# One ScalarE copy for all readers of a product bank in the block inverse of a gated DeltaNet layer

## The chip, the core and the metric

The kernel runs on one core of a Trainium2 chip. The metric is device time in microseconds (us), the median of several executions; lower is better. The core has five engines that run side by side, each through its own queue in order: TensorE (PE; its weight loads are shown as PEld), VectorE (DVE), ScalarE (ACT), GpSimd (POOL) and SyncE (SP), which issues the DMAs. They meet at semaphores.

## The reference

One decoder layer on 2048 tokens of width 1024: a gated DeltaNet mixer with 8 heads in chunks of 64 tokens and a memory attention with 4 heads, one output projection, a layer norm, a squared-ReLU MLP of width 4096, a second layer norm. What matters here is the triangular solve of each chunk:

```python
decay = jnp.exp(jnp.where(causal, gc[..., :, None] - gc[..., None, :], -jnp.inf))
lower = jnp.where(strict, jnp.einsum('bnhcd,bnhsd->bnhcs', k_beta, kc) * decay, 0.0)
a_mat = jnp.eye(CHUNK, dtype=f32) + lower
u = lax.linalg.triangular_solve(a_mat, v_beta, left_side=True, lower=True, unit_diagonal=True)
w = lax.linalg.triangular_solve(a_mat, k_beta * jnp.exp(gc)[..., None], left_side=True,
                                lower=True, unit_diagonal=True)
...
def step(state, inp):
    qd, kd, u_c, w_c, a_c, dc = inp
    v_new = u_c - jnp.einsum('bhcd,bhde->bhce', w_c, state)
    o = jnp.einsum('bhcd,bhde->bhce', qd, state) + jnp.einsum('bhcs,bhse->bhce', a_c, v_new)
    state = state * dc[..., None, None] + jnp.einsum('bhcd,bhce->bhde', kd, v_new)
    return state, o
```

The kernel inverts the unit lower triangular matrix itself, in chunks of 128 tokens, instead of solving twice.

## The kernel before

The tokens are cut into four blocks of 512 (`TB`), each of which holds four chunks (`NC`) of 128 rows. For two blocks at a time the program runs the mixer of each block, the output projection (`out_seven`), and the MLP (`ff1`, `ff2`) with one level of Strassen's scheme. A mixer goes over the 8 heads: `dense` projects q, k and v, `gdn_a` builds the chunks' matrices and calls `invert`, `gdn_b` runs the recurrence over the state. So there are 4 x 8 = 32 calls of `invert`. Head t's projections, head t-1's inverse and head t-2's recurrence are recorded in one turn of the loop, together with the gates, the memory heads and sums of weights for the MLP.

Nothing is issued where it is written. Every call goes into a `Recorder` (L190), which notes for each operation the earlier operations that it depends on: a write against earlier readers and writers of the same tile, a read against earlier writers, told apart by `part` keys and, in SBUF, by partitions and columns (`Ref.mask`). Two reads of one tile make no edge there. `Recorder.cost` (L250) gives each operation a time, `LAT`, `LAT_FROM` and `MARGIN` (L33 to L35) the hand-over between engines, and `Recorder.issue` (L291) plays the engines' queues as a list scheduler: of the operations that are ready on an engine it takes the one recorded first. The order that comes out is the order in which the engines get their instructions; the semaphores are placed afterwards by the framework from what the tiles share. A tile's name in the profile is the name given to it in the code; most lines are that of the one call in `issue` (L402), so groups are told apart by tiles.

`invert` (L851) takes L, four chunks of 128 x 128 whose strictly lower triangle counts, and returns the inverse in Y. It builds up from blocks of 16 to 32 to 64 to 128 rows:

- `Lq` holds the four 32 x 32 diagonal blocks of each chunk, copied by ScalarE from L with the chunk index innermost; two VectorE operations make `Lc` of it, and 15 steps of three VectorE operations each (`B`, `Xc`) eliminate within the blocks of 16. `ZT` and `Z` are the result and its transpose.
- First product pair, blocks of 16: `pq` = LB x ZT, copied to `Q`; `pp` = XB x Q, subtracted from `ZT`.
- `ZP`, the first 64 columns of the same tile `Lq`, receives packed blocks of ZT. `X32` and `X64` (in the `inv` tiles, which are zero outside their blocks) receive the diagonal blocks of Z: of four copies for each, GpSimd makes two and VectorE two. ScalarE copies ZT's diagonal blocks into Y.
- Second pair, blocks of 32: `pq` = L32 x ZP, copied to Q; `pb` (the bank `pp`) = X32 x Q. This bank has five readers: a VectorE transpose of its upper half into the second half of `Lq`, two VectorE multiplications by -1 and two ScalarE activations with scale -1, each of a 32 x 64 block into Y. Two VectorE multiplications by -1 carry the transposed blocks into X64.
- Third pair, blocks of 64: `YP` is packed from Y by one VectorE and one ScalarE copy; `pq` = LP x YP, copied to Q; `pp` = X64 x Q, whose two halves VectorE and ScalarE write, negated, into Y.

`gdn_a` goes on with the transposes of v, and `gdn_b` multiplies by Y.

The bank of each product is one tile of a PSUM pool (`ga0` or `ga1` by the head's parity, one buffer each).

Of the kernel before, what the change touches and what calls it, by code (L numbers as in the profile page):

```python
# [10 lines left out]
AF = mybir.ActivationFunctionType  # L11
# [3 lines left out]
P = 128  # L15
TB = 512
NC = TB // P
# [14 lines left out]

LAT = {("PE", "PE"): 0, ("DVE", "POOL"): 190, ("ACT", "POOL"): 215, ("PE", "POOL"): 350, ("DVE", "DVE"): 130, ("ACT", "ACT"): 155, ("POOL", "POOL"): 100}  # L33
LAT_FROM = {"PE": 200, "DVE": 130, "ACT": 135, "POOL": 75, "SP": 60}
MARGIN = 100  # L35
DRAIN, SWITCH = {"DVE": 90, "ACT": 100, "POOL": 98}, 0


# [145 lines left out]

class Op:
    __slots__ = ("i", "eng", "fn", "args", "kw", "dur", "extra", "succ", "npred", "ready", "start", "end", "load", "last",
                 "bufs", "prio", "quads", "cols", "late", "lhs")


class Recorder:  # L190
# [15 lines left out]
    def add(self, eng, fn, name, args, kw):  # L206
        o = Op()
        o.i, o.eng, o.fn, o.args, o.kw = len(self.ops), eng, fn, args, kw
        o.succ, o.npred, o.ready, o.extra = [], 0, 0, 0
        o.prio = o.i + self.shift  # L210
        wr = [v for k, v in kw.items() if k in ("out", "accum_out")]
        rd = [v for k, v in kw.items() if k not in ("out", "accum_out")]
        rest = list(args)
        if "out" not in kw and rest:
            wr.append(rest.pop(0))
        rd += rest
        wr = [v for v in wr if isinstance(v, Ref)]
        rd = [v for v in rd if isinstance(v, Ref)]
        o.dur = self.cost(o, name, wr, rd, args, kw)

        o.quads = {("r" if v in rd else "w", v.buf.psum): v.p0 // 32 for v in wr + rd[::-1]}
        preds = {}
        for refs, is_w in ((rd, False), (wr, True)):
            for r in refs:
                parts, free = r.mask()
                for q, qw, qk, qp, qf in r.buf.log:
                    if (is_w or qw) and (qk is None or r.keys is None or qk & r.keys) and qp & parts and qf & free:
                        preds[q.i] = q
        for refs, is_w in ((rd, False), (wr, True)):
            for r in refs:  # L230
                log = r.buf.log
                parts, free = r.mask()
                if is_w:
                    log[:] = [e for e in log if not ((e[2] == r.keys or r.keys is None) and e[3] & ~parts == 0
                                                     and e[4] & ~free == 0)]
                log.append((o, is_w, r.keys, parts, free))
        if eng == "SP" and self.gate is not None:
            preds[self.gate.i] = self.gate
        for q in preds.values():
            q.succ.append(o)  # L240
        o.npred = len(preds)
        o.bufs = list({id(r.buf): r.buf for r in rd + wr}.values())
        for b in o.bufs:
            if b.first is None:
                b.first = o.i
            b.users += 1
        self.ops.append(o)
# [43 lines left out]
    def issue(self):  # L291
# [7 lines left out]
        quads, cols = {e: {} for e in DRAIN}, P  # L299
# [40 lines left out]
        out = []  # L340
        fed = 0.0
        while True:
# [3 lines left out]
            for e in engs:  # L346
                if avail[e]:
                    t = free[e]
                elif soon[e]:
                    t = max(free[e], soon[e][0][0])  # L350
# [6 lines left out]
            t, e = best  # L357
            while soon[e] and soon[e][0][0] <= t:
                r, i, o = heapq.heappop(soon[e])
                heapq.heappush(avail[e], (o.prio, i, o))  # L360
            o = heapq.heappop(avail[e])[2]
            if e == "PE":
                if o.cols != cols:
                    t += SWITCH
                    cols = o.cols
                t = max(t, fed + o.load)
                fed = t + o.dur - o.last
            if e in DRAIN:
                at = quads[e]
                if any(at.get(k, q) != q for k, q in o.quads.items()):  # L370
                    t = max(t, free[e] + DRAIN[e])
# [7 lines left out]
            for s in o.succ:  # L379
                lat = LAT.get((e, s.eng), LAT_FROM[e])  # L380
                if e == "PE" and lat and o.last < 60:
                    lat += 65 if o.last > 30 else 130
                if lat:
                    lat += MARGIN + (s.load if s.eng == "PE" and s.lhs in o.bufs else 0)
                s.ready = max(s.ready, o.end + lat)
                s.npred -= 1
                if s.npred == 0:
                    pending.append(s)
# [30 lines left out]
def hybrid_layer(  # L419
# [24 lines left out]
    nc = tc.nc  # L444
# [21 lines left out]
    def small(name, shape, bufs=3, dt=F32):  # L466
        return rec.buf(sm, shape, dt, name, bufs, name)
# [15 lines left out]
    half = cst.tile([P, 2], F32, name="half")  # L483
# [21 lines left out]
    nc = rec  # L505
# [344 lines left out]

    def invert(L, par):  # L851

        Lq = small("Lq", [P, 32, NC], 2)
        for q in range(4):
            r = slice(32 * q, 32 * q + 32)
            nc.scalar.copy(out=Lq[r].rearrange("p f c -> p c f"), in_=L[r, :, 32 * q:32 * q + 32])
            nc.gpsimd.tensor_copy(inv["LB"][r, :, r].rearrange("p u (k f) -> p u k f", k=2),
                                  L[r, :, 32 * q:32 * q + 16].rearrange("p (k u) f -> p u k f", k=2))
        L32, LP = inv["L32"], inv["LP"]
        for p in range(2):  # L860
# [4 lines left out]
        nc.gpsimd.tensor_copy(LP[64:, :, :64].part(0), L[64:, 0:2, :64])  # L865
        nc.vector.tensor_copy(LP[:64, :, 64:].part(1), L[64:, 2:4, :64])
        Lc = small("Lc", [P, 16, NC], 2)
        nc.vector.tensor_scalar_mul(Lc, Lq[:, 0:16], half[:, 0:1])
        nc.vector.scalar_tensor_tensor(out=Lc, in0=Lq[:, 16:32], scalar=half[:, 1:2], in1=Lc,
                                       op0=ALU.mult, op1=ALU.add)  # L870
        Xc = small("Xc", [P, 16, NC], 2)
        nc.vector.tensor_copy(Xc, i16.unsqueeze(2).to_broadcast([P, 16, NC]))
# [1 line left out]
        for j in range(15):  # L874
# [3 lines left out]
                                    in1=Lc[:, j:j + 1].to_broadcast([P, w, NC]), op=ALU.mult)  # L878
            nc.vector.tensor_tensor(out=Xc[:, :w], in0=Xc[:, :w], in1=B[:, :w], op=ALU.subtract)
        Z = small("Z32", [P, NC, 32], 2)  # L880
        for hf in range(2):
# [6 lines left out]
                                       in1=Z[:, 0:2, 0:16], op0=ALU.mult, op1=ALU.add)  # L888
# [25 lines left out]
        nc.vector.tensor_tensor(out=zt, in0=zt, in1=pp.rearrange("p (u k f) -> p u k f", u=2, k=2), op=ALU.subtract)  # L914


        ZP = Lq.rearrange("p f c -> p (f c)")[:, :64].rearrange("p (c f) -> p c f", c=2)
        Z = small("Z32", [P, NC, 32], 2)
        for p in range(2):
            odd = slice(64 * p + 32, 64 * p + 64)  # L920
# [1 line left out]
            nc.scalar.copy(out=ZP[odd].part(2 * p), in_=ZT[odd, 0:2])  # L922
        nc.vector.transpose(Z.rearrange("p c f -> p (c f)"), ZT.rearrange("p c f -> p (c f)"))
        for p in range(2):
            for u, eng in ((0, nc.gpsimd), (1, nc.vector)):
                q = quads[2 * p + u]
                eng.tensor_copy(X32[q, :, q].part((u, p)), Z[64 * p:64 * p + 32, 2 * u:2 * u + 2])
        for p in range(2):
            for u, eng in ((0, nc.gpsimd), (1, nc.vector)):
                q = quads[2 * u + p]  # L930
                eng.tensor_copy(X64[q, :, q].part((u, p)), Z[quads[p], 2 * u:2 * u + 2])
        for r in quads:
            nc.scalar.copy(out=Y3[r, :, r], in_=ZT[r])

# [5 lines left out]
        pp = pb.rearrange("p (c f) -> p c f", c=2)  # L940
        for c in range(2):
            nc.tensor.matmul(pp[:, c], X32[:, c], Q[:, 64 + c * 32:64 + (c + 1) * 32].part(1), start=True, stop=True)
        tr = Lq.rearrange("p f c -> p (f c)")[:64, 64:].part("t")
        nc.vector.transpose(tr, pb[:64])
        for p in (1, 0):
            o = Y3[64 * p:64 * p + 32, :, 64 * p + 32:64 * p + 64]
            nc.vector.tensor_scalar_mul(o[:, 2:4], pp[quads[2 * p + 1]], -1.0)
            nc.scalar.activation(o[:, 0:2], pp[quads[2 * p]], AF.Copy, scale=-1.0)
        tr = tr.rearrange("p (c f) -> p c f", c=2)
        for u in range(2):  # L950
            nc.vector.tensor_scalar_mul(X64[quads[2 * u + 1], :, quads[2 * u]].part((u, 2)), tr[quads[u]].part("t"), -1.0)

        YP = small("YP", [P, 2, 64], 1)
        nc.vector.tensor_copy(YP[:64].part(1), Y3[64:, 2:4, 64:])
# [874 lines left out]
```

## Time and profile before

| what | before |
|---|---|
| median of the runs | 2762.95 us (2762.62 to 2763.29, 3 runs) |
| the profiled execution | 2760.71 us |
| its span, first to last instruction | 2759.0 us |
| mean granted TensorE clock | 0.997 |
| HBM read / written | 436.54 / 174.65 MB |

The span is what the profile shows; the time of an execution has a little around it. In the profile, busy times are those in which an engine worked on an instruction of the program, and "idle before" is the time an engine stood still just before an instruction, with the instruction that released it behind the arrow. A group's row gives out <- in by the names of the tiles, the shape, the count, the busy time and the mean of one in ns. In a timeline, the first column is the start, the second the duration of that instruction or run of instructions. A busy TensorE is not one at its peak, since its matmuls are pipelined and their ends are modelled.

### The profile page before, as it was taken

The page shows a single profiled execution, that of the slowest core. Times are in us where ns is not written, and L with a number is a line of the kernel's source. Part 1 is how long each engine was busy: PE and PEld are TensorE (multiplying, and loading weights), DVE is VectorE, ACT ScalarE, POOL GpSimd, SP SyncE. Part 2 cuts the span into 40 slices and gives each one's busy share as a digit, 9 for nine tenths or more (in the row PEclk, how much of TensorE's full clock was granted, in tenths as well). Part 3 has the DMA queues.
Part 4 walks back from the last instruction along what each step waited for, and adds up shares of the span by engine and source line. Part 5 has one row for each costly group of instructions (what it writes and reads, how often), then busy time and mean ns, then how long its engine had stood idle before and what let it go on. Part 6 is the DMA issues. An engine that isn't in the chain of part 4 may idle for free.

```text
span 2759.0 us, 42405 instructions
## 1 busy us (share of the span) xinstructions
PE 2719.8 (99%) x13589; PEld 2267.0 (82%) x13589; DVE 2112.2 (77%) x5652; ACT 1642.3 (60%) x4082; POOL 403.7 (15%) x1030
## 2 busy tenths in 40 slices
PE   9999999999999999999999999999999999999998
PEld 7888888887788888888888888888887788888887
DVE  7889889998777777665778887888978665657575
ACT  7678767676485556334446676677855655544342
POOL 3233223321000000000023321223201000000000
PEclk9999999999999999999999999999999999999999
DMA  8565558876788888766754344444578744477673
GB/s 327 207 234 205 215 182 288 290 258 228 269 284 302 280 285 297 268 211 205 265 209 149 138 155 174 169 147 159 206 251 280 249 145 152 163 252 243 205 239 116
DMA packets 208543, 613.99 MB, mean 223 GB/s; under 512 B 23072, under 2 KB 32192, under 8 KB 188352
## 3 DMA queue, kind: packets, MB, share of 16 engines
q1 hardware_dynamic: 207888, 611.23, 63.5%
q8 instruction: 107, 1.75, 0.2%
q14 instruction: 116, 0.95, 0.1%
q10 hardware_dynamic: 432, 0.05, 0.0%
HBM read 436.54 MB, written 174.65 MB: 222 GB/s over the span
## 4 chain that ended last, share of the span: by engine, by line
PE 88%; ACT 7%; DVE 4%; issue 1%; POOL 1%; DMA 0%; DVEq 0%; SPq 0%; POOLq 0%; ACTq 0%
PE f2A L402 13%; PE fA L402 12%; PE ao L402 8%; PE f2C L402 6%; PE fC L402 6%; PE az L402 5%; PE aq L402 5%; PE av L402 5%; PE ak L402 5%; PE f2B L402 3%; PE fB L402 3%; PE amq L402 3%; PE pc L402 3%; PE po L402 2%; PE pkq L402 1%
## 5 line engine op out<-in xcount | busy, mean ns | idle before, releaser
L402 DVE TENSOR_TENSOR whl<-wraw,whl 128x512 fp32r<-128x512 f32 (+2 forms) x294 | 257.2, 884 | 109.4 <-ACT whl L402 107.0
L402 ACT CAST whl<-wraw 128x512 fp32r<-128x512 f32 (+2 forms) x294 | 226.5, 780 | 158.0 <-PE fC L402 52.0
L402 PE MATMUL fA<-B,whl 128*128 128x512 f32 x1152 | 277.2, 389 | 1.8 <-ACT B L402 1.5
L402 ACT CAST X<-X 128x1024 fp32r<-128x1024 f32 x118 | 123.9, 1052 | 236.2 <-DMA X<-xsc 196.2
L402 PE MATMUL f2A<-whl,X 128*128 128x512 f32 x1152 | 262.1, 389 | 0.0
L402 PEld LDWEIGHTS fA<-B,whl 128*128 128x128 f32 x1152 | 216.1, 188 | 47.5 <-ACT B L402 1.9
L402 PEld LDWEIGHTS f2A<-whl,X 128*128 128x128 f32 x1152 | 216.2, 188 | 44.9
L402 DVE TENSOR_TENSOR X<-X,X 128x1024 fp32r<-128x1024 f32 x118 | 144.2, 1223 | 129.0 <-ACT X L402 128.8
L402 PE MATMUL aq<-T,whl 128*128 128x512 f32 x768 | 214.3, 408 | 10.0 <-ACT T L402 5.5
L402 PE MATMUL az<-T,whl 128*128 128x512 f32 x768 | 213.0, 406 | 0.0
L402 PE MATMUL ak<-T,whl 128*128 128x512 f32 x768 | 211.4, 406 | 0.0
L402 PE MATMUL av<-T,whl 128*128 128x512 f32 x768 | 210.4, 404 | 0.0
L402 PE MATMUL fC<-B,whl 128*128 128x512 f32 x768 | 185.4, 389 | 0.3 <-DVE B L402 0.3
L402 PE MATMUL f2C<-whl,X 128*128 128x512 f32 x768 | 174.7, 389 | 0.0
L402 PEld LDWEIGHTS fC<-B,whl 128*128 128x128 f32 x768 | 144.1, 188 | 30.7 <-DVE B L402 0.8
L402 PEld LDWEIGHTS f2C<-whl,X 128*128 128x128 f32 x768 | 144.1, 188 | 29.9
L402 PEld LDWEIGHTS aq<-T,whl 128*128 128x128 f32 x768 | 136.5, 191 | 32.7 <-ACT T L402 5.5
L402 POOL TENSOR_SCALAR ve<-mv 128x1 f32<-128x1 f32 x34 | 16.4, 483 | 962.0 <-DVE mv L402 961.5
L402 PEld LDWEIGHTS av<-T,whl 128*128 128x128 f32 x768 | 137.3, 189 | 22.7
L402 PEld LDWEIGHTS ak<-T,whl 128*128 128x128 f32 x768 | 136.4, 189 | 23.5
L402 PEld LDWEIGHTS az<-T,whl 128*128 128x128 f32 x768 | 135.9, 189 | 21.6
L402 PE MATMUL ao<-whl,X 128*128 128x512 f32 x528 | 140.1, 404 | 3.5 <-DVE whl L402 1.3
(287 smaller groups left out, 6300.8 us busy)
## 6 DMA issues: line engine op xcount, KB each, us to landing
whl<-wsc SPq DMA_DIRECT2D x108, 1024.0 KB, 4.8
wraw<-in_w_ff_dram SPq DMA_DIRECT2D x106, 512.0 KB, 4.5
X<-xsc SPq DMA_DIRECT2D x96, 512.0 KB, 3.9
wsc<-whl SPq DMA_DIRECT2D x36, 1024.0 KB, 5.2
whl<-tsc SPq DMA_DIRECT2D x64, 512.0 KB, 4.7
xsc<-hB SPq DMA_DIRECT2D x96, 256.0 KB, 3.4
xo<-cat SPq DMA_DIRECT2D x80, 256.0 KB, 3.9
wraw<-in_w_in_dram SPq DMA_DIRECT2D x35, 512.0 KB, 5.9
```

Source lines behind the costliest of these rows:

```text
L402: o.fn(*[res(a) for a in o.args], **{k: res(v) for k, v in o.kw.items()})
```

## The change

Five things are changed.

1. `Lq` gets the chunk index outermost, so that ScalarE's copies into it are contiguous; `Lc` is made from a permuted view `Lf` of it.
2. The four copies of Z's diagonal blocks into `X32` are all VectorE's, the four into `X64` all GpSimd's.
3. The bank `pb` has one reader, a ScalarE activation with scale -1 that writes all of it into the second half of `Lq` (`Nf`). The transpose (now into the first half, where ZP was), the two VectorE and the two ScalarE copies into Y read that; they and the two copies into X64 are plain copies without a factor.
4. In the recorder, a read of a PSUM tile gets an edge from each earlier read of it by another engine, if there is none yet (`turns`).
5. In the scheduler such an edge counts 40 ns (`TURN`) after the earlier reader's end.

```diff
--- before.py
+++ after.py
@@ -32,7 +32,7 @@
 
 LAT = {("PE", "PE"): 0, ("DVE", "POOL"): 190, ("ACT", "POOL"): 215, ("PE", "POOL"): 350, ("DVE", "DVE"): 130, ("ACT", "ACT"): 155, ("POOL", "POOL"): 100}
 LAT_FROM = {"PE": 200, "DVE": 130, "ACT": 135, "POOL": 75, "SP": 60}
-MARGIN = 100
+MARGIN, TURN = 100, 40
 DRAIN, SWITCH = {"DVE": 90, "ACT": 100, "POOL": 98}, 0
 
 
@@ -184,7 +184,7 @@
 
 class Op:
     __slots__ = ("i", "eng", "fn", "args", "kw", "dur", "extra", "succ", "npred", "ready", "start", "end", "load", "last",
-                 "bufs", "prio", "quads", "cols", "late", "lhs")
+                 "bufs", "turns", "prio", "quads", "cols", "late", "lhs")
 
 
 class Recorder:
@@ -206,7 +206,7 @@
     def add(self, eng, fn, name, args, kw):
         o = Op()
         o.i, o.eng, o.fn, o.args, o.kw = len(self.ops), eng, fn, args, kw
-        o.succ, o.npred, o.ready, o.extra = [], 0, 0, 0
+        o.succ, o.npred, o.ready, o.extra, o.turns = [], 0, 0, 0, set()
         o.prio = o.i + self.shift
         wr = [v for k, v in kw.items() if k in ("out", "accum_out")]
         rd = [v for k, v in kw.items() if k not in ("out", "accum_out")]
@@ -219,13 +219,15 @@
         o.dur = self.cost(o, name, wr, rd, args, kw)
 
         o.quads = {("r" if v in rd else "w", v.buf.psum): v.p0 // 32 for v in wr + rd[::-1]}
-        preds = {}
+        preds, turns = {}, {}
         for refs, is_w in ((rd, False), (wr, True)):
             for r in refs:
                 parts, free = r.mask()
                 for q, qw, qk, qp, qf in r.buf.log:
                     if (is_w or qw) and (qk is None or r.keys is None or qk & r.keys) and qp & parts and qf & free:
                         preds[q.i] = q
+                    elif r.buf.psum and q.eng != eng and not is_w and not qw:
+                        turns[q.i] = q
         for refs, is_w in ((rd, False), (wr, True)):
             for r in refs:
                 log = r.buf.log
@@ -236,6 +238,10 @@
                 log.append((o, is_w, r.keys, parts, free))
         if eng == "SP" and self.gate is not None:
             preds[self.gate.i] = self.gate
+        for i, q in turns.items():
+            if i not in preds:
+                preds[i] = q
+                q.turns.add(o.i)
         for q in preds.values():
             q.succ.append(o)
         o.npred = len(preds)
@@ -382,7 +388,7 @@
                     lat += 65 if o.last > 30 else 130
                 if lat:
                     lat += MARGIN + (s.load if s.eng == "PE" and s.lhs in o.bufs else 0)
-                s.ready = max(s.ready, o.end + lat)
+                s.ready = max(s.ready, o.end + (TURN if s.i in o.turns else lat))
                 s.npred -= 1
                 if s.npred == 0:
                     pending.append(s)
@@ -850,10 +856,10 @@
 
     def invert(L, par):
 
-        Lq = small("Lq", [P, 32, NC], 2)
+        Lq = small("Lq", [P, NC, 32], 2)
         for q in range(4):
             r = slice(32 * q, 32 * q + 32)
-            nc.scalar.copy(out=Lq[r].rearrange("p f c -> p c f"), in_=L[r, :, 32 * q:32 * q + 32])
+            nc.scalar.copy(out=Lq[r], in_=L[r, :, 32 * q:32 * q + 32])
             nc.gpsimd.tensor_copy(inv["LB"][r, :, r].rearrange("p u (k f) -> p u k f", k=2),
                                   L[r, :, 32 * q:32 * q + 16].rearrange("p (k u) f -> p u k f", k=2))
         L32, LP = inv["L32"], inv["LP"]
@@ -865,8 +871,9 @@
         nc.gpsimd.tensor_copy(LP[64:, :, :64].part(0), L[64:, 0:2, :64])
         nc.vector.tensor_copy(LP[:64, :, 64:].part(1), L[64:, 2:4, :64])
         Lc = small("Lc", [P, 16, NC], 2)
-        nc.vector.tensor_scalar_mul(Lc, Lq[:, 0:16], half[:, 0:1])
-        nc.vector.scalar_tensor_tensor(out=Lc, in0=Lq[:, 16:32], scalar=half[:, 1:2], in1=Lc,
+        Lf = Lq.rearrange("p c f -> p f c")
+        nc.vector.tensor_scalar_mul(Lc, Lf[:, 0:16], half[:, 0:1])
+        nc.vector.scalar_tensor_tensor(out=Lc, in0=Lf[:, 16:32], scalar=half[:, 1:2], in1=Lc,
                                        op0=ALU.mult, op1=ALU.add)
         Xc = small("Xc", [P, 16, NC], 2)
         nc.vector.tensor_copy(Xc, i16.unsqueeze(2).to_broadcast([P, 16, NC]))
@@ -914,7 +921,7 @@
         nc.vector.tensor_tensor(out=zt, in0=zt, in1=pp.rearrange("p (u k f) -> p u k f", u=2, k=2), op=ALU.subtract)
 
 
-        ZP = Lq.rearrange("p f c -> p (f c)")[:, :64].rearrange("p (c f) -> p c f", c=2)
+        ZP = Lq.rearrange("p c f -> p (c f)")[:, :64].rearrange("p (c f) -> p c f", c=2)
         Z = small("Z32", [P, NC, 32], 2)
         for p in range(2):
             odd = slice(64 * p + 32, 64 * p + 64)
@@ -922,13 +929,13 @@
             nc.scalar.copy(out=ZP[odd].part(2 * p), in_=ZT[odd, 0:2])
         nc.vector.transpose(Z.rearrange("p c f -> p (c f)"), ZT.rearrange("p c f -> p (c f)"))
         for p in range(2):
-            for u, eng in ((0, nc.gpsimd), (1, nc.vector)):
+            for u in range(2):
                 q = quads[2 * p + u]
-                eng.tensor_copy(X32[q, :, q].part((u, p)), Z[64 * p:64 * p + 32, 2 * u:2 * u + 2])
+                nc.vector.tensor_copy(X32[q, :, q].part((u, p)), Z[64 * p:64 * p + 32, 2 * u:2 * u + 2])
         for p in range(2):
-            for u, eng in ((0, nc.gpsimd), (1, nc.vector)):
+            for u in range(2):
                 q = quads[2 * u + p]
-                eng.tensor_copy(X64[q, :, q].part((u, p)), Z[quads[p], 2 * u:2 * u + 2])
+                nc.gpsimd.tensor_copy(X64[q, :, q].part((u, p)), Z[quads[p], 2 * u:2 * u + 2])
         for r in quads:
             nc.scalar.copy(out=Y3[r, :, r], in_=ZT[r])
 
@@ -940,15 +947,18 @@
         pp = pb.rearrange("p (c f) -> p c f", c=2)
         for c in range(2):
             nc.tensor.matmul(pp[:, c], X32[:, c], Q[:, 64 + c * 32:64 + (c + 1) * 32].part(1), start=True, stop=True)
-        tr = Lq.rearrange("p f c -> p (f c)")[:64, 64:].part("t")
-        nc.vector.transpose(tr, pb[:64])
+        Nf = Lq.rearrange("p c f -> p (c f)")[:, 64:]
+        nc.scalar.activation(Nf, pb, AF.Copy, scale=-1.0)
+        tr = Lq.rearrange("p c f -> p (c f)")[:64, :64]
+        nc.vector.transpose(tr, Nf[:64])
+        N3 = Nf.rearrange("p (c f) -> p c f", c=2)
         for p in (1, 0):
             o = Y3[64 * p:64 * p + 32, :, 64 * p + 32:64 * p + 64]
-            nc.vector.tensor_scalar_mul(o[:, 2:4], pp[quads[2 * p + 1]], -1.0)
-            nc.scalar.activation(o[:, 0:2], pp[quads[2 * p]], AF.Copy, scale=-1.0)
+            nc.vector.tensor_copy(o[:, 2:4], N3[quads[2 * p + 1]])
+            nc.scalar.copy(out=o[:, 0:2], in_=N3[quads[2 * p]])
         tr = tr.rearrange("p (c f) -> p c f", c=2)
         for u in range(2):
-            nc.vector.tensor_scalar_mul(X64[quads[2 * u + 1], :, quads[2 * u]].part((u, 2)), tr[quads[u]].part("t"), -1.0)
+            nc.vector.tensor_copy(X64[quads[2 * u + 1], :, quads[2 * u]].part((u, 2)), tr[quads[u]])
 
         YP = small("YP", [P, 2, 64], 1)
         nc.vector.tensor_copy(YP[:64].part(1), Y3[64:, 2:4, 64:])
```

## The prediction

> **What bounds the kernel now.** I read the page first: which engine fills the span, and which one the chain of waits runs along.
>
> ```profile
> span 2759.0 us, 42405 instructions
> PE 2719.8 (99%) x13589; PEld 2267.0 (82%) x13589; DVE 2112.2 (77%) x5652; ACT 1642.3 (60%) x4082; POOL 403.7 (15%) x1030
> PE 88%; ACT 7%; DVE 4%; issue 1%; POOL 1%; DMA 0%; DVEq 0%; SPq 0%; POOLq 0%; ACTq 0%
> ```
>
> TensorE is busy for 2719.8 of 2759.0 us, so 39.2 us of the span is all that any edit off TensorE can win. The change adds no matmul and removes none. Its worth is therefore not the time of the copies it edits but the part of those 39.2 us that such copies cause. Second I cut the span into stages: the mixers with the inverses run at 60 to 730 and 1330 to 2080 us, the MLPs in the rest.
>
> ```profile
> core 0: us, PE busy (x) PEld busy (x) DVE busy (x) ACT busy (x) POOL busy (x), PEclk, DMA share, GB/s
> 60.00:730.00 670.00, 655.02 (x3654) 552.70 (x3653) 587.72 (x2149) 478.27 (x1500) 182.28 (x451) 0.99 0.67 237
> 1330.00:2080.00 750.00, 745.79 (x4060) 628.05 (x4059) 611.61 (x2172) 480.32 (x1533) 167.94 (x462) 1.00 0.52 184
> ```
>
> TensorE idles 670.00 - 655.02 = 15.0 us in the first mixer stretch and 4.2 us in the second; the granted clock is 0.99 and 1.00, so no clock is to be won. Third, the waits of TensorE over the whole span, to see which are the inverse's own.
>
> ```profile
> PE aq L402 <- DVE Bc L402: 4.5, 1, 4.5
> PE ao L402 <- ACT whl L402: 2.9, 2, 2.6
> PE pmT L402 <- DVE pm L402: 1.7, 1, 1.7
> PE pq L402 <- DVE YP L402: 1.4, 5, 0.5
> PE pq L402 <- ACT YP L402: 1.3, 2, 0.7
> PE pq L402 <- DVE ZT L402: 0.5, 1, 0.5
> PE ptv L402 <- ACT Y L402: 0.4, 2, 0.2
> PE pq L402 <- POOL inv L402: 0.3, 1, 0.3
> PE pp L402 <- ACT inv L402: 0.3, 1, 0.3
> PE pp L402 <- issue: 0.2, 1, 0.2
> ```
>
> (Total us, times, longest.) The inverse's own waits are the last seven: 1.4 + 1.3 + 0.5 + 0.4 + 0.3 + 0.3 + 0.2 = 4.4 us in 32 inverses. The largest pair, 2.7 us, is the third product (LP times YP) waiting for the two halves of YP, which come out of the bank that the change edits. The three rows at the top are single events of 4.5, 2.6 and 1.7 us in which TensorE waits for work queued on VectorE or ScalarE.
>
> Fourth, the timeline of one inverse from that bank to that wait:
>
> ```profile
> 446.20 0.60 PE L402 MATMUL pp<-inv 128*128 128x32 f32 x4 [0.19 <-issue]
> 446.84 0.24 DVE L402 STREAM_TRANSPOSE Lq<-pp 64x64 f32<-64x64 f32 x1 [1.53 <-PE pp L402]
> 447.26 0.21 ACT L402 ACTIVATE Y<-pp 32x64 f32<-32x64 f32 x1
> 447.51 0.23 DVE L402 TENSOR_SCALAR Y<-pp 32x64 f32<-32x64 f32 x1 [0.43 <-ACT Y L402]
> 447.77 0.21 ACT L402 ACTIVATE Y<-pp 32x64 f32<-32x64 f32 x1 [0.29 <-DVE Y L402]
> 448.02 0.21 DVE L402 TENSOR_SCALAR Y<-pp 32x64 f32<-32x64 f32 x1 [0.28 <-ACT Y L402]
> 448.31 0.29 ACT L402 COPY YP<-Y 64x128 f32<-64x128 f32 x1
> 448.67 0.22 DVE L402 COPY YP<-Y 64x128 f32<-64x128 f32 x1
> 449.03 0.63 PE L402 MATMUL pq<-YP,inv 128*128 128x64 f32 x4 [0.29 <-DVE YP L402]
> ```
>
> The reader is to see a strict alternation: VectorE, ScalarE, VectorE, ScalarE, VectorE, each starting when the other has let go of the bank, although they write different blocks. From the product's end (446.80) to the end of the last YP copy (448.89) pass 2.09 us. The planner's model has no edge between two readers of a bank, so it plans them side by side and sends TensorE to the third product too early.
>
> **The change part by part.** The durations come from these grouped rows (count | busy, mean ns | idle before):
>
> ```profile
> L402 ACT COPY Lq<-dl 32x128 f32<-32x128 f32 x128 | 53.4, 417 | 4.1 <-DVE dl L402 2.9
> L402 ACT COPY Y<-ZT 32x128 f32<-32x128 f32 x128 | 37.9, 296 | 1.9
> L402 ACT COPY inv<-pq 128x64 f32<-128x64 f32 x32 | 6.7, 208 | 1.4 <-PE pq L402 0.7
> L402 ACT COPY Lq<-ZT 32x64 f32<-32x64 f32 x64 | 15.5, 243 | 12.9 <-DVE ZT L402 12.1
> L402 DVE TENSOR_SCALAR Y<-pp 32x64 f32<-32x64 f32 x64 | 14.2, 222 | 7.7 <-ACT Y L402 6.1
> L402 ACT ACTIVATE Y<-pp 32x64 f32<-32x64 f32 x64 | 13.7, 214 | 18.4 <-PE pp L402 10.3 <-DVE Lq L402 4.9 <-DVE Y L402 1.9
> L402 DVE COPY inv<-Z 32x64 f32<-32x64 f32 x128 | 27.3, 214 | 2.7
> L402 POOL COPY inv<-Z 32x64 f32<-32x64 f32 x128 | 35.0, 274 | 59.8 <-DVE Z L402 44.8 <-DVE Bc L402 6.2 <-DVE Xc L402 3.2
> L402 DVE TENSOR_SCALAR Lc<-Lq,half 128x64 f32<-128x64 f32 x32 | 8.0, 250 | 4.5 <-ACT Lq L402 4.1
> L402 DVE TENSOR_SCALAR Z<-Xc,half 128x64 f32<-128x64 f32 x64 | 17.4, 324 | 0.3
> ```
>
> *The negated copy.* One ScalarE read of 128x64 from the bank is new; its nearest row is the copy inv<-pq of the same shape, 208 ns, and the bounds are 208 and 243 (ScalarE's dearest 32x64 copy). The five later readers then take SBUF, where the alternation is not needed. The chain becomes 446.80 + 0.04 (the gap before the transpose now) + 0.21 for the copy + 0.1 hand-over; then VectorE runs transpose 0.24, Y 0.21, Y 0.21, YP 0.22 = 0.88 while ScalarE runs Y 0.24, Y 0.24, YP 0.29 = 0.77. That makes 1.23 us against 2.09, a gain of 0.86 us. If the planner puts the transpose or a foreign piece of work between, I bound it at 0.3 to 1.1 (the lower end: the two VectorE waits of 0.28 and 0.29 lose one and the new copy costs its 0.21 beside a shorter queue).
>
> The Trainium skill's page "PSUM — Partial Sum Buffer", section "PSUM bank collisions raise a hardware error", says that two engines may access one bank at the same time if they are in different 32-partition quadrants. Here the two engines do read different quadrants, so by that rule the old readers could have run side by side, and the extra copy would be a pure addition of 0.21 us per inverse. The rows above show the program taking turns all the same, with 0.28 and 0.29 us of waiting, so the sum goes by the rows.
>
> *Queue time given back.* The bracketed idle on the Y rows is 6.1 us on VectorE and 4.9 + 1.9 us on ScalarE: 12.9 us in which an in-order queue stood still for a turn, with casts, the conv and the splits of weights queued behind.
>
> *Layout of Lq.* ScalarE now writes contiguous rows: 417 ns falls towards 296, the same shape written contiguously; four copies in a row per inverse, so the head is 0.48 us earlier, and ScalarE saves 128 x 0.121 = 15.5 us against 32 x 0.21 + 64 x 0.03 = 8.6 us added. VectorE's two Lc operations now read with a stride. The row that is nearest is Z<-Xc, which reads permuted: 324 against 250, so +0.07 each, 0.15 per inverse, 4.7 us in all on an engine that is 77% busy. It is covered by the other 23%, except where TensorE waits on VectorE's backlog (the 4.5 us row): there one or two inverses are open, +0.2.
>
> *32-row copies to VectorE, 64-row copies to GpSimd.* Both engines keep four copies each per inverse, so the queues carry the same. The 32-row ones feed the next product: the last is done 4 x 0.214 = 0.86 us after Z where GpSimd's two took 0.55 and VectorE's came in the midst of four. Bounds -0.3 to +0.3; I take 0. The 64-row ones take 4 x 0.274 = 1.10 us on GpSimd and are first needed two products later, after the 2.09 us above, which is what hides them; without that cover they would cost 1.10 per inverse.
>
> *The planner's edge of 40 ns* makes the order wait where readers of a bank alternate; it is no instruction. Among the operations of the mixers it acts on the inverse's last bank (VectorE, then ScalarE), where 0.4 us of TensorE's wait (ptv for Y) hangs on it.
>
> **The sum.** (1) The inverse's own 4.4 us: I take four fifths, 3.5, since a gain of 0.86 us is above the longest of these waits (0.7). (2) The end of a mixer stretch, where TensorE has run out of other work and follows the last head's recurrence:
>
> ```profile
> 702.32 0.49 PE L402 MATMUL pc<-state,ck 128*128 128x128 f32 x2 [0.22 <-DVE state L402]
> 703.25 0.49 PE L402 MATMUL pc<-R,Y 128*128 128x128 f32 x2 [0.22 <-DVE R L402]
> 704.15 0.49 PE L402 MATMUL pc<-vt,kd 128*128 128x128 f32 x2 [0.41 <-ACT vt L402]
> 707.49 2.07 PE L402 MATMUL ao<-whl,xh 128*128 128x512 f32 x4 [2.64 <-ACT whl L402]
> ```
>
> 3.49 us of idle in four rows. The last inverse ends 0.48 + 0.86 - 0.15 = 1.19 us earlier, so the recurrence does too: 1.2 us. (3) The 12.9 us of queue time: TensorE's other waits on VectorE and ScalarE shrink by about a tenth of it, 1.4 us with the rounding (an estimate; ends 0 and 4.5, the largest single row). (4) The strided reads, +0.2. Together -3.5 - 1.2 - 1.4 + 0.2 = -5.9 us. The profiled execution took 2760.71 us (span 2759.0 and 1.7 around it), so 2754.8 for it; the median of the runs stands 2762.95 - 2760.71 = 2.24 us above it, which gives 2757.0.
>
> **The rivals.**
>
> *A: hidden anyway.* The new plan spends the shorter chain by sending TensorE to the third product earlier, so that it waits as before, and single events like 4.5 or 1.7 us merely move. For it: in 32 inverses only 7 waits on YP show. Against it: the planner's model was wrong by the turns, and now needs none on this bank. It keeps about 2 of the 4.4 us: 2761.
>
> *B: slower, by ScalarE as the gate.* Every later reader, VectorE's transpose too, now stands behind one copy in ScalarE's queue, which is 478.27 / 670.00 = 71% busy in the mixers. If the copy starts late, both halves of YP are late at once; the longest such wait seen is 0.7 us. At 0.7 for half of the 32 inverses that is 11.2 us, less the 2.7 now there: +8.5, so 2771. It decides from the point where the copy starts more than 0.9 us after the product's end in most inverses. Against it: ScalarE already held half of the old chain.
>
> *C: the turns go on in SBUF.* Copy, transposed block and ZP share one tile; if waits go by tile and not by block, the alternation stays and the copy is on top: 0.21 + 0.1 per inverse, up to 9.9 us if TensorE pays all, about half of it likely: 2767. Against it: GpSimd's and VectorE's copies into one inv tile were free to overlap, their idle being for Z and not for each other.
>
> **How the numbers follow.** About 0.2%, 5.5 us, is what a measurement of this kernel can tell from no change. My forecast has 0.60, of which 0.45 lies beyond 5.5 us and 0.15 short of it; A 0.23; B 0.11; C 0.06. Faster 0.46 (with a little of A where the moved events happen to vanish), same 0.37, slower 0.17. The range: at the lower end all 4.4, the 3.5 of the stretch's end and both other top rows (4.5 + 1.7) go, -14, 2749; at the upper end C and two thirds of B are taken in, 2768. The forecast's own range is 2751 to 2760.
>
> **What would show it.** Right: between the bank's product and YP no alternation, one negated copy of about 0.21 us, and some 1.2 to 1.5 us to YP's end; the two pq<-YP rows of TensorE's waits together under 1 us; Lq<-dl near 296 ns; Lc near 320; TensorE's busy time unchanged within 1 us and its idle near 33. Wrong: a new row of pq or pp waiting for the copy (B), ScalarE and VectorE still alternating (C), or a large single wait in a place that the inverse doesn't touch, which would mean that the new order, and not the shorter chain, set the time.

## The result and the profile after

| what | before | after |
|---|---|---|
| median of the runs | 2762.78 us (2759.85 to 2763.55, 10 runs) | 2755.19 us (2753.55 to 2757.94, 10 runs) |
| the profiled execution, and its span | 2760.71 us, 2759.0 us | 2755.49 us, 2753.8 us |
| mean granted TensorE clock | 0.997 | 0.997 |

The ratio is 0.9975 with a 95% interval of 0.9966 to 0.9983: faster by 7.6 us, a little over a quarter of a per cent, where 5.9 were forecast. The page of the changed kernel:

```profile
span 2753.8 us, 42437 instructions
PE 2716.6 (99%) x13589; PEld 2271.7 (82%) x13589; DVE 2111.9 (77%) x5652; ACT 1633.5 (59%) x4114; POOL 408.0 (15%) x1030
```

TensorE's idle time is 2753.8 - 2716.6 = 37.2 us against 39.2, so only 2.0 of the 5.2 us of span are idle time that the page counts. The other 3.2 are busy time, though the same 13589 matmuls ran. My reading is that, since a matmul's end is modelled, a short stall behind it is booked as busy. I therefore also took, from the trace, the difference between the starts of each two consecutive matmuls and booked it to the later one. These sums by tile add up to TensorE's time from its first matmul to its last and need no modelled end. In them pq, the first product of each pair, falls from 54.3 to 48.2 us (4.6 of it at the third pair's, LP times YP, from 22.3 to 17.7), pmT by 2.1, the MLP's fA by 3.0, pp by 1.0; against that, ao, the output projection, rises from 231.3 to 234.7 and pkq from 52.3 to 55.5.

Some of the waits of TensorE over the whole span, after (total us, times, longest):

```profile
PE ao L408 <- DVE whl L408: 4.1, 4, 2.4
PE aq L408 <- DVE Xc L408: 3.9, 1, 3.9
PE ao L408 <- ACT whl L408: 3.1, 2, 2.6
PE pkq L408 <- DVE at L408: 1.4, 3, 0.9
PE ptv L408 <- ACT Y L408: 0.3, 2, 0.2
```

No row of pq or pp is in the whole answer; of the inverse's 4.4 us only ptv's 0.3 remains. The large single waits are still there, some in other places: 3.9 for 4.5 at aq, 2.6 at ao as before, and a new one of 2.4. The longest of all, 5.8 us of aq for T near the start of the span (5.5 before), is not shown above.

The edited bank to the third product in the timeline, after (start, duration):

```profile
450.26 0.60 PE L408 MATMUL pp<-inv 128*128 128x32 f32 x4
450.90 0.22 ACT L408 ACTIVATE Lq<-pp 128x64 f32<-128x64 f32 x1
451.69 0.24 ACT L408 COPY Y<-Lq 32x64 f32<-32x64 f32 x1
451.87 0.22 DVE L408 STREAM_TRANSPOSE Lq<-Lq 64x64 f32<-64x64 f32 x1
452.13 0.40 DVE L408 COPY Y<-Lq 32x64 f32<-32x64 f32 x2
452.35 0.23 ACT L408 COPY Y<-Lq 32x64 f32<-32x64 f32 x1
452.55 0.42 DVE L408 COPY inv<-Lq 32x64 f32<-32x64 f32 x2
452.61 0.30 ACT L408 COPY YP<-Y 64x128 f32<-64x128 f32 x1
453.00 0.22 DVE L408 COPY YP<-Y 64x128 f32<-64x128 f32 x1
453.36 0.63 PE L408 MATMUL pq<-YP,inv 128*128 128x64 f32 x4
```

The alternation is gone: ScalarE's second Y copy (452.35) runs beside VectorE's two (452.13 to 452.53), and no row carries a bracketed wait. But the way is not shorter: from the product's end at 450.86 to the end of YP at 453.22 pass 2.36 us, against 2.09 in the timeline before, because the plan puts other work between (ScalarE does something else from 451.12 to 451.69). Over all 32 inverses the mean is 2.59 us after and 2.29 before. What changed is that YP is ready before TensorE comes.

The groups that answer to those of before (count | busy, mean ns | idle before):

```profile
L408 ACT COPY Lq<-dl 32x128 f32<-32x128 f32 x128 | 37.6, 294 | 3.1 <-DVE dl L408 1.6
L408 ACT ACTIVATE Lq<-pp 128x64 f32<-128x64 f32 x32 | 7.1, 221 | 9.7 <-PE pp L408 9.3
L408 ACT COPY Y<-Lq 32x64 f32<-32x64 f32 x64 | 15.5, 242 | 1.6
L408 DVE COPY Y<-Lq 32x64 f32<-32x64 f32 x64 | 13.1, 205 | 2.0
L408 DVE TENSOR_SCALAR Lc<-Lq,half 128x64 f32<-128x64 f32 x32 | 8.7, 272 | 1.8 <-ACT Lq L408 1.6
L408 PEld LDWEIGHTS pq<-YP,inv 128*128 128x128 f32 x128 | 18.1, 190 | 4.7 <-issue 1.9 <-POOL halo L408 0.7 <-POOL m L408 0.3
```

The last row has a counterpart before that the forecast did not look at:

```profile
L402 PEld LDWEIGHTS pq<-YP,inv 128*128 128x128 f32 x128 | 17.3, 190 | 10.4 <-ACT YP L402 5.5 <-issue 2.4 <-ACT dl L402 0.4
```

The third product's weight loads waited 10.4 us before and 4.7 now, and the wait for YP has gone from them. The rows of its matmuls showed 2.7 us of waiting for YP, while the time from start to start fell by 4.6: the matmul rows alone understated the wait.

### The profile page after: what moved, and what is told of

Same layout as the page of the kernel before. It is cut to its first block, busy times and chain, and to the rows that moved or that the text cites. A ratio compares the mean times of both kernels' runs of the same rounds, so it can differ in the third digit from the quotient of the medians.

```text
span 2753.8 us, 42437 instructions
## 1 busy us (share of the span) xinstructions
PE 2716.6 (99%) x13589; PEld 2271.7 (82%) x13589; DVE 2111.9 (77%) x5652; ACT 1633.5 (59%) x4114; POOL 408.0 (15%) x1030
## 4 chain that ended last, share of the span: by engine, by line
PE 93%; ACT 3%; DVE 3%; issue 1%; POOL 0%; DMA 0%; DVEq 0%; SPq 0%; POOLq 0%; ACTq 0%
PE f2A L408 13%; PE fA L408 12%; PE ao L408 8%; PE aq L408 6%; PE ak L408 6%; PE f2C L408 6%; PE fC L408 6%; PE av L408 6%; PE az L408 6%; PE f2B L408 3%; PE fB L408 3%; PE amq L408 3%; PE pc L408 3%; PE po L408 2%; PE pkq L408 2%; PE pq L408 1%
```

## The experiments

Each kernel was timed beside the kernel before on the same chip.

**One part at a time.** Turns only: the changed kernel's recorder and scheduler with the old `invert`.

```diff
...
+                    elif r.buf.psum and q.eng != eng and not is_w and not qw:
+                        turns[q.i] = q
...
+        for i, q in turns.items():
+            if i not in preds:
+                preds[i] = q
+                q.turns.add(o.i)
...
+                s.ready = max(s.ready, o.end + (TURN if s.i in o.turns else lat))
```

> Only the recorder's edges between readers of one PSUM tile and their 40 ns in the scheduler are added; every instruction is as before. Theory P (the plan: TensorE was sent to the third product too early because the planner did not know that the five readers of the bank take turns): the planner now knows it, so the two pq<-YP rows of TensorE's waits fall from 2.7 to under 1 us with the alternation itself still there, and the time falls by 3 to 6 us, to about 2758. Theory C (the chain: fewer and faster steps of VectorE and ScalarE): nothing on the engines is shorter, so 0 to -1 us. Theory R (any new order moves single waits of 2 to 5 us about): anything within 4 us either way, and the pq<-YP rows need not go.

Measured: 2767.49 us, ratio 1.0018 (1.0009 to 1.0027). The planner was told of the turns and no time was won: pq's sum rose to 58.3 us. Some of TensorE's waits at pq in that kernel:

```profile
PE pq L408 <- DVE ZT L408: 4.2, 1, 4.2
PE pq L408 <- DVE Lq L408: 2.2, 1, 2.2
PE pq L408 <- DVE YP L408: 0.5, 1, 0.5
PE pq L408 <- ACT YP L408: 0.3, 1, 0.3
```

Half of theory P came true. The two waits for YP fell from 2.7 to 0.8 us, as it said, and the third product, the pq behind that bank, from 22.3 to 20.1 us. The first two products, whose banks have no such turn, rose from 32.0 to 38.2 us, with single waits of 4.2 and 2.2 us that were 0.5 and none before, and the time did not fall. The time is also 5 us off the kernel before, beyond theory R's 4.

The changed kernel without the edges:

```diff
...
-                    elif r.buf.psum and q.eng != eng and not is_w and not qw:
-                        turns[q.i] = q
...
-        for i, q in turns.items():
-            if i not in preds:
-                preds[i] = q
-                q.turns.add(o.i)
...
-                s.ready = max(s.ready, o.end + (TURN if s.i in o.turns else lat))
+                s.ready = max(s.ready, o.end + lat)
```

> The changed kernel without the new edges: new layout, placement, one negated copy. Theory P: the edited bank has one reader from PSUM, so no edge is needed there; only the inverse's last bank is again planned without its turn, so ptv's waits for Y stay near 0.4 us and the time is within 1 us of the changed kernel's, about 2756. Theory C: the same, since the instructions are the same, 2755 to 2756. Theory R: up to 4 us off the changed kernel, either way.

Measured: 2763.51 us, ratio 1.0005 (0.9996 to 1.0014). The same instructions as the changed kernel, 8.3 us slower. pq's sum is 49.8 us, so most of the gain at the inverse is there, but ao's is 238.4 against 231.3 before and takes it all back. P and C both said 2755 to 2756, R at most 4 us off; all three miss.

The negated copy alone, in the old layout:

```diff
-        nc.vector.transpose(tr, pb[:64])
+        nc.scalar.activation(Nf, pb, AF.Copy, scale=-1.0)
+        nc.vector.transpose(tr, Nf[:64])
...
-            nc.vector.tensor_scalar_mul(o[:, 2:4], pp[quads[2 * p + 1]], -1.0)
-            nc.scalar.activation(o[:, 0:2], pp[quads[2 * p]], AF.Copy, scale=-1.0)
+            nc.vector.tensor_copy(o[:, 2:4], N3[quads[2 * p + 1]])
+            nc.scalar.copy(out=o[:, 0:2], in_=N3[quads[2 * p]])
...
```

> Before with the one negated ScalarE copy and the plain copies behind it alone; old layout of Lq, old placement, no new edges. Theory P: the unplanned turns on this bank are gone, so pq<-YP waits fall under 1 us and the time by 3 to 6 us. Theory C: the part of the chain behind the product gets 0.3 to 0.9 us shorter, with 2 to 4 us of gain. Theory R: within 4 us either way.

Measured: 2770.71 us, ratio 1.0030 (1.0018 to 1.0042), the opposite of what P and C expected of the time, and more than R's 4 us. TensorE's waits of pq for YP fell to 0.4 us, as P said, and pq's sum fell (49.6 us); ao rose to 242.1, pp to 50.0.

The layout alone:

```diff
-        Lq = small("Lq", [P, 32, NC], 2)
+        Lq = small("Lq", [P, NC, 32], 2)
...
```

> Before with the new layout of Lq alone (contiguous ScalarE copies of 0.30 in place of 0.42 us, strided reads for Lc, +0.02 to +0.05 us each). Theory P: the alternation of readers stays and so do the pq<-YP waits, 2 to 3 us; the planner counts the copies at the same price as before, so the drift of the plan shrinks by 0.48 us per inverse at its head and the pq<-ZT wait of 0.5 us goes: 0 to -2 us. Theory C: 15 us of ScalarE time less, -2 to -4 us. Theory R: within 4 us either way.

Measured: 2762.57 us, ratio 1.0002 (0.9993 to 1.0011). ScalarE's busy time fell from 1642.3 to 1627.7 us in the profile, and the time did not move, so C's 2 to 4 us for ScalarE's time did not show.

The placement alone:

```diff
-            for u, eng in ((0, nc.gpsimd), (1, nc.vector)):
+            for u in range(2):
                 q = quads[2 * p + u]
-                eng.tensor_copy(X32[q, :, q].part((u, p)), Z[64 * p:64 * p + 32, 2 * u:2 * u + 2])
+                nc.vector.tensor_copy(X32[q, :, q].part((u, p)), Z[64 * p:64 * p + 32, 2 * u:2 * u + 2])
...
-                eng.tensor_copy(X64[q, :, q].part((u, p)), Z[quads[p], 2 * u:2 * u + 2])
+                nc.gpsimd.tensor_copy(X64[q, :, q].part((u, p)), Z[quads[p], 2 * u:2 * u + 2])
```

> Before with the placement alone: the four copies into X32 on VectorE, the four into X64 on GpSimd; margin 100, all else as before. If the placement shortens the way to the second pair's product: pp's sum falls from 47.3 to about 46 us and GpSimd's waits show no pp waiting for inv copies; pq's sum stays at 54 to 59 us, since the bank's five readers are untouched; the time from 2760 to 2772 by the new plan. If it only moves work: pp and pq unchanged within 1 us.

Measured: 2772.15 us, ratio 1.0037 (1.0024 to 1.0051). pp's sum went from 47.3 to 47.8 us, so the placement did not shorten the way to it. The slower time stands at pq (58.1) and ao (236.2), which moved by more than the 1 us expected; I put that down to the new plan, from this one plan.

**The plan itself.** No part brought the gain, and two parts cost several us where their own products got faster or stayed. So I changed the plan and nothing else: the scheduler's margin for a hand-over between engines, 100 ns, to 104 and to 96. Every instruction of the engines stays (their counts are the same in the pages); only the order that the list scheduler makes differs, and with it the semaphores.

```diff
-MARGIN = 100
+MARGIN = 104
```

> The kernel before with the scheduler's hand-over margin at 104 in place of 100 ns: no instruction differs, only the order it makes. Theory S (two terms: the negated copy takes 4 to 6 us off TensorE's time at the pq products, in every plan; the output projection's ao products, at the ends of the mixer stretches, scatter by several us with any new plan): pq's start-to-start sum stays at 54 to 58 us as before (54.3), ao's lies anywhere between 231 and 242, and the time anywhere from -1 to +9 us. Theory L (the new edges do something of their own that saves 8 us): this kernel has none of them, the time stays within 1 us of before.

> The kernel before with the margin at 96 ns. Theory S: as with 104, pq 54 to 58 us, ao 231 to 242, the time -1 to +9 us and not the same as with 104. Theory L: within 1 us of before.

Measured: 2767.27 us with 104 (ratio 1.0017, 1.0008 to 1.0025) and 2777.32 us with 96 (1.0054, 1.0041 to 1.0066). The same program spans 15 us over three plans, and the margin of 100 is the best of the three. The expected ranges ended at +9 us; the second plan is at +15, so the scatter was set too small. pq's sum was 53.4 and 58.6 us, each 0.6 us outside theory S's 54 to 58; theory L's 1 us is missed by both.

```diff
-MARGIN, TURN = 100, 40
+MARGIN, TURN = 104, 40
```

> The changed kernel with the margin at 104 ns. Theory S: pq's sum stays at 48 to 50 us as in the changed kernel (48.2), ao's scatters (234.7 there), so the time goes from 2755 to 2766, likely above the changed kernel's. Theory L: the edges are there, so the time stays at 2754 to 2757.

> The changed kernel with the margin at 96 ns. Theory S: pq 48 to 50 us, ao scatters, time 2755 to 2766. Theory L: 2754 to 2757.

Measured: 2748.93 us with 104 (ratio 0.9952, 0.9938 to 0.9965) and 2751.65 us with 96 (0.9963, 0.9950 to 0.9975), both faster than the changed kernel where I had expected slower, and below theory L's 2754 to 2757. The changed kernel with 104 beats both kernels of this case. pq's sums, 47.2 and 48.8, came close to theory S's 48 to 50; ao's, 229.9 and 230.1, were the lowest of all plans.

**Do the new edges matter?** The changed kernel without them, in two more plans, and the copy alone in one more:

```diff
-MARGIN, TURN = 100, 40
+MARGIN = 104
...
```

> The changed kernel without the new edges, margin 104 ns. Theory K (the negated copy alone accounts for the fall at pq, the edges are worth nothing on average): pq's sum 47 to 50 us, and the time anywhere from 2748 to 2764, so that the three plans without edges (100: 2763.5; 104; 96) average within 5 us of the three with them (2755.2, 2748.9, 2751.7: 2751.9). Theory E (the edges on the inverse's last bank bring several us in every plan): pq as in K, the time 2757 to 2767, the average of the three 7 us or more above 2751.9, and the ptv or pc sums are larger than with edges.

> The changed kernel without the new edges, margin 96 ns. Theory K: pq 47 to 50 us, time 2748 to 2764. Theory E: pq as in K, time 2757 to 2767.

> Before with the negated copy and the plain copies behind it alone, margin 104 ns; its like with 100 took 2770.7 us. Theory K: pq 47 to 50 us against 53.4 in the kernel before with this margin, and the time about 5 us under that kernel's 2767.3, give or take the scatter of a new plan (6 us): 2756 to 2768. If the layout and the placement are needed for the gain: pq 47 to 50 us but pp at 50 us or more, as it was with margin 100, and the time 2767 to 2772.

Measured: 2758.05 us (0.9986, 0.9978 to 0.9995), 2761.11 us (0.9994, 0.9985 to 1.0003) and, for the copy alone, 2763.39 us (1.0001, 0.9992 to 1.0010). With the first run of no edges, the three plans without edges average 2760.9 us and the three with them 2751.9: 9.0 apart, and by pairs 8.3, 9.1 and 9.5. That is what theory E said of the time, and more than theory K's 5 us. It does not hold where E put it: ptv's sums (18.9, 18.2, 18.8 without, 18.5, 18.7, 18.8 with) are no larger without the edges, and neither are pc's on average. The copy alone came as theory K said of it (pq 47.9, the time in its range); beside the kernel before with the same margin it is 3.9 us faster with 104 and was 7.9 us slower with 100, so what it is worth in time depends on the plan.

The sums, from one profile of each kernel (us; the median time of the runs in the last column):

```
kernel                      pq (third)     pp      ao   memory   dense   half     time
before                    54.3    22.3   47.3   231.3     72.7   732.9   13.7   2762.8
before, margin 104        53.4    23.4   47.9   230.5     69.2   733.3   10.2   2767.3
before, margin 96         58.6    25.5   51.3   235.6     69.1   733.5   17.1   2777.3
edges alone               58.3    20.1   48.7   232.4     68.9   733.2   23.9   2767.5
layout alone              54.9    23.4   46.3   239.0     70.1   733.1   23.9   2762.6
placement alone           58.1    25.9   47.8   236.2     70.8   734.6   13.7   2772.2
copy alone                49.6    18.8   50.0   242.1     69.2   734.0   27.3   2770.7
copy alone, margin 104    47.9    17.7   50.0   231.9     71.3   731.6   10.2   2763.4
no edges                  49.8    16.8   48.8   238.4     71.8   733.7   27.3   2763.5
no edges, margin 104      48.3    17.5   47.2   232.7     70.1   730.4   10.2   2758.1
no edges, margin 96       51.3    21.9   47.2   239.5     70.6   730.7   23.9   2761.1
after                     48.2    17.7   46.3   234.7     69.4   731.0   13.7   2755.2
after, margin 104         47.2    16.7   48.1   229.9     67.6   733.3   20.5   2748.9
after, margin 96          48.8    17.5   48.0   230.1     67.8   731.5   10.2   2751.7
```

(third: of pq, the third product, LP times YP; memory: pmT, pmo and sps; dense: aq, ak, av, az and amq; half: the time between TensorE's first and last matmul in which its granted clock was 0.50.) The first column is the one that sorts: the six kernels without the copy lie from 53.4 to 58.6, mean 56.3; the eight with it from 47.2 to 51.3, mean 48.9. There is no overlap, in fourteen different plans. Of the 7.4 us between the means, 5.3 lie at the third product, the one behind the edited bank. There the five kernels with neither copy nor edges lie from 22.3 to 25.9, the eight with the copy from 16.7 to 21.9, and the edges alone at 20.1, in between. Of the other columns none of pp, ao, memory and dense separates the kernels with the copy from those without.

**The granted clock.** One thing that moves the time from plan to plan stands in none of these sums as such. In every profile the granted clock falls to 0.50 for a few stretches of 3.4 to 10.2 us, most of them between 636 and 743 us and between 2016 and 2095 us, around the ends of the mixer stretches. One of copy alone, and the time behind it:

```profile
core 0: us, PE busy (x) PEld busy (x) DVE busy (x) ACT busy (x) POOL busy (x), PEclk, DMA share, GB/s
2088.56:2095.38 6.82, 5.26 (x12) 4.18 (x13) 6.82 (x9) 4.76 (x6) 0.00 (x0) 0.50 1.04 400
2095.38:2102.20 6.82, 6.82 (x31) 5.61 (x30) 6.82 (x11) 2.23 (x4) 0.00 (x0) 1.00 0.40 129
```

Within such stretches two consecutive matmuls of ao start about 427 ns apart in the median, outside them 227, in every one of the fourteen profiles. So a microsecond at half clock costs a busy TensorE about 0.47 us (an estimate from these two figures). The pair of this case is not touched by it: both kernels have 13.7 us at half clock. Copy alone, no edges, layout alone and edges alone have 23.9 to 27.3. By the same estimate about 6 us of ao's rise of 10.8 us in copy alone, and about 6 of the 7.1 in no edges, are the clock's. It moves the same kernel too: copy alone with margin 104 took 2758.6 to 2763.5 us in the five runs with a mean clock of 0.997 and 2763.7 to 2767.3 in the three with 0.995. The plans at margin 96 before (17.1 us) and of the placement (13.7) are slow without it. Why one plan gets more of these stretches than another was not tested.

## Why the prediction was right, and where not

**That the pq waits are the place: right. That TensorE's idle of 39.2 us is all that can be won: wrong.** The two rows of pq waiting for YP, 2.7 us, are gone in the changed kernel, and pq's sum is lower with the copy in every plan. But only 2.0 of the 5.2 us of span came out of TensorE's idle time, and 3.2 out of what the page books as busy, where the prediction had busy time unchanged within 1 us and the idle near 33 us (it is 37.2).

**Term (1), 3.5 us at the inverse: the mechanism right, the size too small.** The inverse's waits fell from 4.4 to 0.3 us, and pq's sum by 6.1 in this pair, 4.6 of it at the third product; the mean over plans is 7.4. I had read the matmuls' own waits (4.4 us) as the whole price. The weight loads' idle before the third product, in the row shown above, is where more of it stood: it fell by 5.7 us.

**The chain of 1.23 us: wrong.** It got no shorter, 2.59 us on average. The step that failed is the tacit one from "each engine has less to wait for" to "YP is done earlier": here the list scheduler filled the freed time with other work, as the timeline above shows. What the runs show is that TensorE comes later relative to YP: from YP's end to the third product pass 0.38 us on average, 0.19 before. My reading is that the copy removes turns that the planner does not know, so that its time for YP holds. Edges alone, where the planner knows the turns and the engines still take them, speaks for it: there too TensorE comes later (0.34 us from YP's end to the third product), and the third product falls by 2.2 us, about half of the 4.6 here. It is one plan, and the reading is not shown beyond that; nor is it shown what the copy adds to the knowledge.

**Term (2), 1.2 us at the end of a mixer stretch: no fall of idle.** The four waits of 0.22, 0.22, 0.41 and 2.64 us are all still there at the same lengths, 3.0 us earlier. The timeline after:

```profile
699.29 0.49 PE L408 MATMUL pc<-state,ck 128*128 128x128 f32 x2 [0.22 <-DVE state L408]
700.22 0.49 PE L408 MATMUL pc<-R,Y 128*128 128x128 f32 x2 [0.22 <-DVE R L408]
701.12 0.49 PE L408 MATMUL pc<-vt,kd 128*128 128x128 f32 x2 [0.41 <-ACT vt L408]
704.46 1.04 PE L408 MATMUL ao<-whl,xh 128*128 128x512 f32 x2 [2.63 <-ACT whl L408]
```

At the second stretch's end new waits stand in their place, the longest 2.44 us at 2076.07 for a split of weights on VectorE:

```profile
2076.07 1.41 PE L408 MATMUL ao<-whl,X 128*128 128x512 f32 x4 [2.44 <-DVE whl L408]
```

At 1942 us of the kernel before, the same aq matmul comes 10.1 us earlier in the changed one; at the start of the second MLP only 2.8 us are left of it. The last head's recurrence and the operands of ao take them back.

**Term (3), queue time: part of the idle went, the gain is not shown.** VectorE's idle before its Y copies fell from 7.7 to 2.0 us, ScalarE's from 18.4 to 1.6; but 9.7 us of ScalarE's now stand before the negated copy. The layout, which gave ScalarE 14.6 us back, moved the time by nothing.

**Term (4), the layout: right.** 294 ns for 296 expected; Lc's two operations went to 272 and 326 ns where I had 320. The placement's 0 was right by pp's sum.

**The edges, taken at nothing but a wait of 0.4 us: wrong.** They are worth 9 us over three pairs of plans of the changed kernel. In the kernel before, one plan, they cost 5, with 10.2 us more at half clock. Of the edges that put an order in the changed program, 32 lie on the inverse's last bank and 4 in the gates, so nearly all are that one turn. Between the two sets of three plans the sums differ at ao by 5.3 us (236.9 to 231.6), in the memory heads by 2.6 and at pq by 1.7, not at ptv. The clock is part of it: the plans without edges have 20.5 us at half clock on average and those with them 14.8, which by the estimate above is about 3 of the 9 us, nearly all of it at ao. It is not all of it, since at margin 104 the clock is the other way round (10.2 without, 20.5 with) and the edges are still 9.1 us apart. How the known turn at Y gets to the output projection was not shown, and remains open; so does whether three pairs are enough, since within each set the plans lie 5 to 6 us apart.

**The rivals.** A (hidden anyway) fell in its mechanism: the pq waits did not come back. Its other half, that single events merely move, is true: a new wait of 2.4 us stands at ao, which was named as a sign of being wrong, and in two of the part kernels ao's rise took the whole gain, though more than half of that rise is the clock's by the estimate above. B (ScalarE as the gate): the copy starts 0.06 us after the product's end in the median, and over 0.9 us in one of 32 inverses, so its point was not reached. C (turns in SBUF): the timeline shows none.

**"No clock is to be won": right for this pair, wrong as a rule.** The means of 0.99 and 1.00 hide the stretches at half clock, of which the fourteen plans have 10 to 27 us.

So the sign and the size came right, the size with luck: term (1) was too small, terms (2) and (3) did not show as such, and the edges were taken at nothing. The inverse's products are worth 7.4 us and the edges about 9, while the scatter of a plan, for which I had single events of up to 4.5 us, is 15 us wide over three plans of the kernel before. At equal margins the change is worth 7.6, 18.3 (2767.27 - 2748.93) and 25.7 us (2777.32 - 2751.65), 17.2 on average; of the three margins, the one that the kernel before came with is the one at which that kernel is best and the change worth least.

## What to carry to other kernels

Where a program's order is planned, judge an edit over several plans: nudge a constant of the planner that changes no instruction, for both versions, before believing a difference of less than half a per cent. Sum the differences between the starts of consecutive matmuls by tile: such a sum shows at once that an edit did its work (pq) and that another place took it back (ao), where busy and idle time show neither. Look at the stretches of half clock in each profile as well, before a part is blamed for a rise. Here a bank with several readers on two engines was better read once; telling the planner that the readers take turns gave, in one plan, about half as much at the product behind it.

## What the runs showed that was not expected

- A change of 4 ns in 100 in the planner's margin moved the same instructions from 2763 to 2767 and 2777 us.
- The plan also moves the clock: the changed kernel without the edges spent 10.2, 23.9 and 27.3 us at half clock in three plans of the same instructions.
- A matmul's wait can be hidden in the profile: TensorE's total idle fell by 2.0 us while the span fell by 5.2, and the weight loads' idle before one group fell by 5.7.
- A ScalarE copy of 32 x 128 elements took 417 ns when it wrote with a stride of four elements and 294 when it wrote contiguously.
